# Conditioning row of the first projection: whole rows of 2048 columns ahead of the weights, and a counter of four

## Chip, cores and metric

One core of one Trainium2 chip. The metric is the device time of one execution in microseconds, taken as the median of several runs.

## What is computed

Two transformer-like blocks run one after the other on 256 tokens of width 1024. Only the head of the first block matters here: a condition vector `c` makes a shift and a scale for the tokens, and the modulated tokens are projected to queries, keys and values.

```
def ada_modulation(c, w, b):
    mod = jax.nn.silu(c) @ w + b
    shift, scale, gate = jnp.split(mod, 3, axis=-1)
    return shift[:, None, :], scale[:, None, :], gate[:, None, :]
...
        shift, scale, gate = ada_modulation(c, ada_w[i, 0], ada_b[i, 0])
        h = x * (1.0 + scale) + shift
        if i % N_MIXERS == 0:
            y = windowed_gqa(h, attn_w_in[j], attn_w_out[j], attn_sinks[j])
```

`ada_w[0, 0]` has 1024 rows of 3072 columns. Shift and scale are its first 2048 columns (8 MB); `attn_w_in` has 1024 rows of 1536 columns (6 MB).

## The kernel before, in words

**The weights' stream.** A `Stream` object `W` holds a list of items in the order of their use. An item is either a weight block (`add`) or a filler with a function of its own (`fill`). `load_to` (line 176) issues each item's DMA on SyncE's queue into one of `NSTAGE = 5` staging tiles `stg` of 1 MB. `split_to` (line 196) divides a weight block into a rounded part `wh` (ScalarE, line 217) and a rest `wl` (VectorE, line 222), in halves of up to 1024 columns, so that `mm3` (lines 389 to 391) can multiply in three passes. `step` (line 228) takes the next item: it loads up to five items ahead, splits blocks that are near, and for a filler calls its function, which multiplies the tile that has landed.

**The first projection.** `ada0(c)` (line 656) makes, for each c of 0 to 7, a filler with the 256 columns of `ada_w` that modulate the 128 channels c: 128 of the shift and 128 of the scale. Its DMA has runs of 128 floats, 512 bytes each. The filler multiplies with `cS` (the condition after silu, as 32 columns of which one is filled) on TensorE (line 671) into `adaps`, and VectorE copies the result to `adaR` (line 673). The items alternate: filler c, block c of `attn_w_in` (768 KB).

In `project` (line 1083) TensorE goes through c = 0 to 7. For each c, `modulate(c)` turns the row of `adaR` into two columns by two small matmuls (line 1075), adds the bias (line 1077), applies them to the transposed tokens `xT` on ScalarE (line 1079), and makes the pair `hH`, `hL` on VectorE (lines 1080, 1081). Then come 18 matmuls of 512 columns: 6 for keys and values (into `gen`) and 12 for queries (into `acc`). `turn_in` transposes the tokens (line 1059). Pieces of another job, the filters `hy` of the second block (lines 976 and 994), are put in at c = 4, 5, 6 and 7. The order of TensorE is the order of the program; the orders of the other engines come from a scheduler.

**After the projection.** The attention follows, and inside it eight fillers of whole rows (line 433) for the next shift and scale, which `fin_ss` hands to `row_cols` (line 485). That sends the row from `adaR` (VectorE, line 440) to DRAM and back as columns `adaC` by two DMAs on GpSimd's queue (lines 489 and 490), and puts the use of the columns (`sst`, lines 569 to 573) on a list with a counter:

```
        GP.dma_start(flat, R[row:64 * n:32, :])
        GP.dma_start(C[:, :n, :], flat.rearrange("(s r) (p k) -> s (r p) k", s=n, k=8).rearrange("s p k -> p s k"))
        W.due.append([LAG, lambda: use(C)])
```

Each `step` counts it down; below zero the use is put into the program. `gate_sums` (line 506) sums partial products for the gate on TensorE (line 502) and adds them to a tile `gate` on VectorE (line 503).

Of the kernel before, what the change touches and what calls it, by code (L numbers as in the profile page):

```python
# [11 lines left out]
F32 = mybir.dt.float32  # L12
F32R = mybir.dt.float32r
I32 = mybir.dt.int32
AF = mybir.ActivationFunctionType
OP = mybir.AluOpType
# [17 lines left out]
GROUPS = [(0,), (1, 2), (3, 4), (5, 6)]  # L34
RANK = [6, 7, 8, 9, 0, 2, 3, 1, 4, 5, 10, 11, 12, 13]
NSTAGE, NPART, NMORE = 5, 4, 6
LAG = 2
QSCALE = float(HD ** -0.5)


# [238 lines left out]
def tile_model(ctx: ExitStack, tc: tile.TileContext, A, out):  # L279
    nc = tc.nc  # L280
    PE, V, SC, GP = nc.tensor, nc.vector, nc.scalar, nc.gpsimd
    cst = ctx.enter_context(tc.tile_pool(name="cst", bufs=1))
# [3 lines left out]
    sml = ctx.enter_context(tc.tile_pool(name="sml", bufs=2))  # L286
    rows = ctx.enter_context(tc.tile_pool(name="rows", bufs=4, space=bass.MemoryType.DRAM))

    W = Stream(tc, stage, parts, NSTAGE, 1)
# [19 lines left out]
    one = K("ones")  # L309
# [14 lines left out]
    cS = cst.tile([128, 8, 32], F32, name="cS")  # L324
    cS2 = cst.tile([128, 8, 32], F32, name="cS2")
    V.memset(cS, 0.0)
    V.memset(cS2, 0.0)
    epsc = cst.tile([128, 3], F32, name="epsc")
    V.memset(epsc[:, 0:1], 1e-5)
    V.memset(epsc[:, 1:2], 1e-6)  # L330
    csil = cst.tile([128, 3, 8], F32, name="csil")
# [65 lines left out]
    psC = pes.enter_context(tc.tile_pool(name="psC", bufs=1, space=PSUM))  # L397
# [4 lines left out]
    def gen():  # L402
        return psB.tile([128, 512], F32, name="gen")
# [233 lines left out]
    def collect(jobs):  # L637

        keep, W.items = W.items, []
        for j in jobs:  # L640
            j()
        got, W.items = W.items, keep
        return got
# [8 lines left out]
            done = want  # L652


    ADA0 = {}
    VCH = ()

    def ada0(c):
        def fn(t):
            tv = t.rearrange("p (j n) -> p j n", j=8)  # L660
            if c in VCH:
                R = sml.tile([128, 256], F32, name="adaQ")
                V.tensor_scalar(R, tv[:, 0, :], csil[:, 0, 0:1], None, op0=OP.mult)
                for j in range(1, 8):
                    V.scalar_tensor_tensor(R, tv[:, j, :], csil[:, 0, j:j + 1], R, op0=OP.mult, op1=OP.add)
                ADA0[c] = R
                return
            ps = psC.tile([128, 512], F32, name="adaps")
            for j in range(8):
                g = j % 4  # L670
                PE.matmul(ps[32 * g:32 * g + 32, :256], cS[:, j, :], tv[:, j, :], start=(j < 4), stop=(j >= 4))
            R = sml.tile([128, 512], F32, name="adaR", bufs=1)
            V.tensor_copy(R[:, :256], ps[:, :256])
            ADA0[c] = R

        ap = A["ada_w"][0, 0][:, 0:2048].rearrange("(p j) (s c n) -> c p j s n", j=8, s=2, n=128)[c]
        W.fill("ada", ap, fn)

    wv, wo = rview("attn_w_in", 0), rview("attn_w_out", 0)
    for k in range(8):  # L680
        ada0(k)
        W.add("attn_in", wv[:, k, :])
    fl = collect([ADA1[0, 1][0], ADA1[0, 0][3]])
    for m in range(4):
        n0, n1 = ((0, 6), (6, 8), (8, 10), (10, 12))[m]
# [345 lines left out]
        hps.close()  # L1031


    W.load_to(1)
    late_loads()

    def attention():
        aes = ExitStack()
        ap = aes.enter_context(tc.tile_pool(name="attn", bufs=1, reuse_waits="tile"))
# [13 lines left out]
        def turn_in(first):  # L1053
# [14 lines left out]
            V.tensor_copy(badd[:, 0], pv[:, 0])  # L1068
            V.tensor_scalar(badd[:, 1], pv[:, 1], 1.0, None, op0=OP.add)

        def modulate(c):
            R = ADA0.pop(c)
            ps = gen()
            for s in range(2):
                PE.matmul(ps[:, s:s + 1], R[:, 128 * s:128 * s + 128], one, start=True, stop=True)
            ab = sml.tile([128, 2], F32, name="ab0")
            V.tensor_add(ab, ps[:, 0:2], badd[:, :, c])
            v = ip.tile([128, 256], F32, name="v0", bufs=2)
            SC.activation(v, xT[:, c, :], AF.Identity, bias=ab[:, 0:1], scale=ab[:, 1:2])
            V.tensor_copy(hH[:, c, :], v)  # L1080
            V.tensor_sub(hL[:, c, :], v, hH[:, c, :].bitcast(F32))

        def project(hy):
            W.step()
            turn_in(True)
            kv = [gen(), gen()]
            modulate(0)
            
            qa = [[accb(), accb()], [accb(), accb()]]
            for c in range(8):  # L1090
                w = W.next("attn_in")
                (qh, ql), (kh, kl) = w.parts

                def rows(ps, t, wh, wl):
                    ts = slice(128 * t, 128 * t + 128)
                    mm3(ps, (hH[:, c, ts], hL[:, c, ts]), (wh, wl), c == 0, c == 7)

                if 0 < c < 7:
                    W.step()
                for t in range(2):  # L1100
                    rows(kv[t], t, kh, kl)
                if c == 0:
                    turn_in(False)
                    W.step()
                if c < 7:
                    modulate(c + 1)
                for g in range(2):
                    sl = slice(512 * g, 512 * g + 512)
                    for t in range(2):
                        rows(qa[g][t], t, qh[:, sl], ql[:, sl])  # L1110
                for _ in range((0, 1, 0, 0, 1, 1, 1, 1)[c]):
                    next(hy)
                if c == 6:
                    nc.sync.dma_start(amask, A["c_amask"])
            return kv, qa
# [1452 lines left out]
```

## Time and profile before

| | us |
|---|---|
| median of 3 runs | 1212.63 (1207.86 to 1213.87) |
| the profiled execution | 1208.85 |
| its span | 1206.8 |
| TensorE busy in the span | 1125.0 (93%) |
| VectorE busy | 776.7 (64%) |
| ScalarE busy | 551.3 (46%) |
| the large DMA queue, share of 16 engines | 70.9% |

The rows below come from the profiled execution. Its own time is 3.8 us under the median of the runs. Times in a timeline count from the start of the span. In a row, `[1.10 <-DVE adaR L673]` says that the engine was idle for 1.10 us before and what ended it.

### The profile page before, as it was taken

The numbers are of one execution on the slowest core, as the hardware profiler recorded it, in microseconds if no ns is written. First come the engines' busy times: TensorE is split into PE (matmuls) and PEld (weight loads), VectorE is DVE, ScalarE is ACT, GpSimd is POOL, SyncE is SP. The second block draws the span as 40 slices with busy tenths as digits, with TensorE's granted clock in tenths as the row PEclk, the third lists the DMA queues.
The fourth block names the chain that finished last, engine by engine and source line by source line (L and its number), as shares of the span: only waits on it lengthen the run. The fifth ranks groups of instructions, "written<-read, shape, count | busy, mean of one in ns | idle before, by whom it ended". The sixth has DMA issues, their size and how long they took to land. (4 is left out here: it accounts for less than half of the span.)

```text
span 1206.8 us, 17360 instructions
## 1 busy us (share of the span) xinstructions
PE 1125.0 (93%) x6618; PEld 821.0 (68%) x6618; DVE 776.7 (64%) x1458; ACT 551.3 (46%) x934; POOL 103.9 (9%) x177
## 2 busy tenths in 40 slices
PE   5999799999989999989999999999999898999974
PEld 3657598989866576548889988888988533335321
DVE  4588788888575885597788769968798621112112
ACT  2456444454457677745445545753665410102111
POOL 6000271000013120010000000100000000000000
PEclk9999899999989999989999999999999999999998
DMA  9988598988694572468879876564326889999994
GB/s 287 323 323 302 187 316 310 331 299 300 208 261 145 164 203 68 146 225 318 284 258 315 279 239 204 186 207 140 123 96 213 356 345 420 420 420 382 342 407 173
DMA packets 146050, 317.57 MB, mean 263 GB/s; under 512 B 8402, under 2 KB 97730, under 8 KB 129576
## 3 DMA queue, kind: packets, MB, share of 16 engines
q1 hardware_dynamic: 138744, 304.17, 70.9%
q0 software_dynamic: 7216, 12.22, 3.3%
q8 instruction: 54, 0.88, 0.3%
q14 instruction: 36, 0.29, 0.1%
HBM read 315.27 MB, written 1.09 MB: 262 GB/s over the span
## 5 line engine op out<-in xcount | busy, mean ns | idle before, releaser
L217 ACT ACTIVATE wh<-stg 128x1024 fp32r<-128x1024 f32 x236 | 241.2, 1042 | 192.4 <-issue 71.3
L222 DVE TENSOR_TENSOR wl<-stg,wh 128x1024 fp32r<-128x1024 f32 x233 | 276.9, 1206 | 72.8 <-ACT wh L217 70.1
L391 PE MATMUL gen<-hH,wl 128*128 128x256 f32 x704 | 198.4, 282 | 4.6 <-DVE wl L222 4.6
L389 PE MATMUL gen<-hH,wh 128*128 128x256 f32 x704 | 199.6, 284 | 3.0 <-ACT hH L847 2.0
L390 PE MATMUL gen<-hL,wh 128*128 128x256 f32 x704 | 197.9, 282 | 1.0 <-DVE hL L851 1.0
L389 PEld LDWEIGHTS gen<-hH,wh 128*128 128x128 f32 x704 | 135.2, 192 | 10.8 <-ACT hH L847 5.3
L391 PEld LDWEIGHTS gen<-hH,wl 128*128 128x128 f32 x704 | 135.1, 192 | 7.3 <-DVE wl L222 7.3
L390 PEld LDWEIGHTS gen<-hL,wh 128*128 128x128 f32 x704 | 135.1, 192 | 2.9 <-POOL zp L1454 0.8
L389 PE MATMUL acc<-wh,mH 128*128 128x512 f32 x256 | 101.2, 395 | 0.0
L391 PE MATMUL acc<-wh,mL 128*128 128x512 f32 x256 | 100.7, 393 | 0.0
L390 PE MATMUL acc<-wl,mH 128*128 128x512 f32 x256 | 100.5, 393 | 0.0
L466 DVE SCALAR_TENSOR_TENSOR adav<-stg,csil,adav 128x1024 f32<-128x1024 f32 (+2 forms) x56 | 79.3, 1415 | 11.6 <-DMA stg<-in_ada_w_dram 10.8
L2393 PE MATMUL mgu<-stg,wl 128*32 128x512 f32 (+2 forms) x256 | 64.4, 625 | 7.1 <-DMA stg<-in_moe_w_up_dram 7.1
L2428 PE MATMUL mmi<-stg,mhT 128*32 128x512 f32 (+2 forms) x256 | 59.1, 598 | 7.3 <-DMA stg<-in_moe_w_down_dram 5.7
L2393 PE MATMUL mgu<-stg,wh 128*32 128x512 f32 (+2 forms) x256 | 64.4, 613 | 0.0
L1499 PE MATMUL gen<-xr,bd 128*128 128x256 f32 (+1 forms) x224 | 60.3, 411 | 1.4 <-DVE xr L1475 1.4
L2438 DVE TENSOR_TENSOR mhid<-mmi,gate 128x512 f32<-128x512 f32 x14 | 9.6, 689 | 80.2 <-PE mmi L2428 80.2
L389 PEld LDWEIGHTS acc<-wh,mH 128*128 128x128 f32 x256 | 48.1, 188 | 11.6 <-issue 0.8
L391 PEld LDWEIGHTS acc<-wh,mL 128*128 128x128 f32 x256 | 48.1, 188 | 10.9 <-issue 0.8
L390 PEld LDWEIGHTS acc<-wl,mH 128*128 128x128 f32 x256 | 48.1, 188 | 10.3 <-DVE wl L222 0.6
L2398 DVE SCALAR_TENSOR_TENSOR mhid<-mgu,mws,mhid 128x512 f32<-128x512 f32 x7 | 5.3, 750 | 70.0 <-PE mgu L2393 70.0
L2393 PEld LDWEIGHTS mgu<-stg,wl 128*32 128x32 f32 (+2 forms) x256 | 18.8, 134 | 44.5 <-issue 32.0
(604 smaller groups left out, 2117.2 us busy)
## 6 DMA issues: line engine op xcount, KB each, us to landing
stg<-in_ada_w_dram SPq DMA_DIRECT2D x72, 1024.0 KB, 6.1
stg<-in_mlp_w_dram SPq DMA_DIRECT2D x64, 1024.0 KB, 6.8
stg<-in_moe_w_up_dram SPq DMA_DIRECT2D x32, 1024.0 KB, 11.0
stg<-in_moe_w_gate_dram SPq DMA_DIRECT2D x32, 1024.0 KB, 11.5
stg<-in_moe_w_down_dram SPq DMA_DIRECT2D x32, 1024.0 KB, 18.1
stg<-in_w_in_dram SPq DMA_DIRECT2D x20, 1024.0 KB, 5.4
stg<-in_rnn_w_in_dram SPq DMA_DIRECT2D x12, 1024.0 KB, 6.3
stg<-in_attn_w_in_dram SPq DMA_DIRECT2D x8, 768.0 KB, 10.3
```

The source lines that it names most:

```text
L217: nc.scalar.activation(h, t[:, sl], AF.Copy)
L222: sub()
L389: PE.matmul(o, ah, bh, start=first, stop=False)
L390: PE.matmul(o, ah, bl, start=False, stop=False)
L391: return PE.matmul(o, al, bh, start=False, stop=last)
L466: V.scalar_tensor_tensor(acc, tv[:, j, :], col[:, k:k + 1], acc, op0=OP.mult, op1=OP.add)
L1499: PE.matmul(pv[c0:c1, q, :], BD[g % 2][:, q, d, o:o + c1 - c0], xr[g][:, kt, :], start=(i == 0), stop=True, skip_group_check=True)
L2393: PE.matmul(ps[sl], gx[c][:, k, o + sl.start:o + sl.stop], t[:, 512 * k:512 * k + 512], start=first, stop=last)
L2398: V.scalar_tensor_tensor(hid, got[1], WS[w], hid, op0=OP.mult, op1=OP.mult)
L2428: PE.matmul(both[h][sl], hT[:, k, sl], t[:, o:o + 512], start=k == 0, stop=k == 3)
L2438: V.tensor_mul(gated, ps, MOD["g5"][:, 512 * h:512 * h + 512])
```

## The change

The eight fillers of 256 columns become eight of whole rows: filler kc holds 2048 columns of the rows 8p + kc, in runs of 8192 bytes, made by the same helper `ada_fill` that the later fillers use. All eight add into one `adaps`, so shift and scale are complete after the eighth only. The first seven stand ahead of the first block of `attn_w_in`, the eighth behind it. One set of four small matmuls with `pick` (four columns, each one on 32 partitions) turns the whole row into all 16 columns, and one addition adds the biases. The loads of the constants and tokens stand behind four tiles where they stood behind one. `LAG` goes from 2 to 4.

```diff
-LAG = 2
+LAG = 4
...
+    pick = cst.tile([128, 4], F32, name="pick")
+    V.memset(pick, 0.0)
+    for g in range(4):
+        V.memset(pick[32 * g:32 * g + 32, g:g + 1], 1.0)
...
-    ADA0 = {}
-    VCH = ()
-
-    def ada0(c):
...
-        ap = A["ada_w"][0, 0][:, 0:2048].rearrange("(p j) (s c n) -> c p j s n", j=8, s=2, n=128)[c]
-        W.fill("ada", ap, fn)
+    ADA0 = []
+    ada_fill("ada", cS, A["ada_w"][0, 0].rearrange("(p k) n -> p k n", k=8), 0, 512, ADA0.append)
+    last = W.items.pop()
 
     wv, wo = rview("attn_w_in", 0), rview("attn_w_out", 0)
     for k in range(8):
-        ada0(k)
         W.add("attn_in", wv[:, k, :])
+        if k == 0:
+            W.items.append(last)
...
-    W.load_to(1)
+    W.load_to(4)
     late_loads()
...
+        ab = ip.tile([128, 2, 8], F32, name="ab0")
+
+        def columns():
+
+            R = ADA0.pop()
+            ps = gen()
+            for k in range(4):
+                PE.matmul(ps[:, 4 * k:4 * k + 4], R[:, 128 * k:128 * k + 128], pick, start=True, stop=True)
+            V.tensor_add(ab.rearrange("p s (h k) -> p s h k", h=2),
+                         ps[:, 0:16].rearrange("p (k s h) -> p s h k", k=4, s=2),
+                         badd.rearrange("p s (h k) -> p s h k", h=2))
+
         def modulate(c):
-            R = ADA0.pop(c)
-            ps = gen()
-            for s in range(2):
-                PE.matmul(ps[:, s:s + 1], R[:, 128 * s:128 * s + 128], one, start=True, stop=True)
-            ab = sml.tile([128, 2], F32, name="ab0")
-            V.tensor_add(ab, ps[:, 0:2], badd[:, :, c])
             v = ip.tile([128, 256], F32, name="v0", bufs=2)
-            SC.activation(v, xT[:, c, :], AF.Identity, bias=ab[:, 0:1], scale=ab[:, 1:2])
+            SC.activation(v, xT[:, c, :], AF.Identity, bias=ab[:, 0, c:c + 1], scale=ab[:, 1, c:c + 1])
...
         def project(hy):
-            W.step()
-            turn_in(True)
+            for k in range(7):
+                W.step(0 if k < 6 else None)
+                if k == 5:
+                    turn_in(True)
+            turn_in(False)
+            w = W.next("attn_in", 0)
+            W.step(0)
+            columns()
             kv = [gen(), gen()]
             modulate(0)
...
             for c in range(8):
-                w = W.next("attn_in")
+                w = W.next("attn_in") if c else w
...
-                if 0 < c < 7:
-                    W.step()
                 for t in range(2):
                     rows(kv[t], t, kh, kl)
-                if c == 0:
-                    turn_in(False)
-                    W.step()
                 if c < 7:
                     modulate(c + 1)
```

What TensorE has at its start, before the change (`adaps` are the fillers, `acc<-csm,xnat` the transposes of tokens, `gen<-csm,adaR` the columns, `gen<-wh,hH` the first projection matmul):

```order
L671 MATMUL adaps<-stg,cS 32x256 x8
L1059 MATMUL acc<-csm,xnat 128x128 x4
L1066 MATMUL gen<-csm,brow 128x16
L1075 MATMUL gen<-csm,adaR 128x1 x2
L389 MATMUL gen<-wh,hH 128x512
```

and with the change, where `gen<-pick,adaR` makes all columns:

```order
L437 MATMUL adaps<-stg,cS 32x512 x24
L1044 MATMUL acc<-csm,xnat 128x128 x4
L1051 MATMUL gen<-csm,brow 128x16
L437 MATMUL adaps<-stg,cS 32x512 x4
L1044 MATMUL acc<-csm,xnat 128x128 x12
L437 MATMUL adaps<-stg,cS 32x512 x4
L1063 MATMUL gen<-pick,adaR 128x4 x4
L393 MATMUL gen<-wh,hH 128x512
```

The first projection matmul has moved from behind one filler to behind eight, and no filler or column matmul stands between the projection's matmuls any more.

On VectorE, with the change, the same place, from the copies of the transposed tokens to the first `hH`, `hL`:

```order
L1046 COPY xT<-acc 128x512
L222 TENSOR_TENSOR wl<-stg,wh 128x1024
L222 TENSOR_TENSOR wl<-stg,wh 128x512
L444 COPY adaR<-adaps 128x512
L1064 TENSOR_TENSOR ab_197<-gen,badd 128x16
L1071 CAST hH<-v_295 128x256
L1072 TENSOR_TENSOR hL<-v_295,hH 128x256
```

The rest of the first weight block (`wl`) stands ahead of the copy of the row, where before it stood behind `hH` and `hL`.

On VectorE, near the end of the attention, before the change (`sst` uses the columns `adaC`, `gate` frees a PSUM bank):

```order
L569 TENSOR_TENSOR sst<-adaC,adb 128x8
L570 SCALAR_TENSOR_TENSOR sst<-adaC,adb 128x8
L503 SCALAR_TENSOR_TENSOR gate<-gen,gate 128x512
L571 TENSOR_TENSOR ab_1083<-sst,gbc 128x8
L573 TENSOR_TENSOR ab_1083<-sst,gbc 128x8
L222 TENSOR_TENSOR wl<-stg,wh 128x1024
```

and with it:

```order
L573 TENSOR_TENSOR sst<-adaC,adb 128x8
L574 SCALAR_TENSOR_TENSOR sst<-adaC,adb 128x8
L575 TENSOR_TENSOR ab_1003<-sst,gbc 128x8
L577 TENSOR_TENSOR ab_1003<-sst,gbc 128x8
L576 TENSOR_TENSOR ab_1003<-ab_1003,sst 128x8
L507 SCALAR_TENSOR_TENSOR gate<-gen,gate 128x512
```

The use of the columns still stands ahead of the gate's sum, with three small operations more between them.

## Rows read from the trace of the kernel before

**Rows 1.** Four stretches: columns are stretch, busy us (count) by engine, clock, DMA share, GB/s.
```profile
2.00:4.00 2.00, 0.00 (x0) 0.00 (x0) 0.17 (x1) 0.24 (x2) 2.00 (x4) 1.00 0.54 131
20.00:30.00 10.00, 8.90 (x64) 6.40 (x63) 5.98 (x10) 4.83 (x7) 4.75 (x9) 1.00 1.16 318
60.00:70.00 10.00, 10.00 (x42) 7.22 (x42) 7.75 (x34) 3.85 (x9) 0.00 (x0) 1.00 1.02 422
70.00:80.00 10.00, 9.74 (x53) 4.77 (x53) 9.20 (x29) 3.99 (x7) 0.00 (x0) 1.00 0.43 150
```

**Rows 2.** Timeline of TensorE: start us, us, line, operation, count, idle before.
```profile
8.15 1.94 PE L671 MATMUL adaps<-stg,cS 128*32 128x256 f32 x16 [8.15 <-DMA stg<-in_ada_w_dram]
...
16.12 0.80 PE L389 MATMUL gen<-wh,hH 128*128 128x512 f32 x1 [2.35 <-ACT wh L217]
...
18.91 0.63 PE L390 MATMUL gen<-wl,hH 128*128 128x512 f32 x1
19.34 0.63 PE L391 MATMUL gen<-wh,hL 128*128 128x512 f32 x1
...
22.46 1.09 PE L671 MATMUL adaps<-stg,cS 128*32 128x256 f32 x16
...
64.67 1.12 PE L994 MATMUL gen<-hw,ha 64*128 64x512 f32 x2
65.72 0.50 PE L389 MATMUL gen<-wh,hH 128*128 128x512 f32 x1
66.06 0.40 PE L390 MATMUL gen<-wl,hH 128*128 128x512 f32 x1
...
69.73 0.40 PE L391 MATMUL acc<-wh,hL 128*128 128x512 f32 x1
70.06 2.84 PE L994 MATMUL gen<-hw,ha 64*128 64x512 f32 x6
```

**Rows 3.** DMA queues and issues, 0 to 30 us: KB each, us to landing.
```profile
q0 software_dynamic: 1088, 0.25, 5.5%
...
stg<-in_ada_w_dram SPq DMA_DIRECT2D x5, 1024.0 KB, 9.9
stg<-in_attn_w_in_dram SPq DMA_DIRECT2D x4, 768.0 KB, 11.8
xnat<-in_x_dram SPq DMA_DIRECT2D x2, 512.0 KB, 6.0
csm<-c_small_dram SPq DMA_DIRECT2D x1, 247.0 KB, 7.1
```

**Rows 4.** Timeline of all engines: from a row's product to its hH.
```profile
15.58 1.83 DVE L222 TENSOR_TENSOR wl<-stg,wh 128x1024 fp32r<-128x1024 f32 x2 [0.20 <-ACT wh L217]
...
24.18 0.42 DVE L673 COPY adaR<-adaps 128x256 f32<-128x256 f32 x1
24.65 0.61 PE L1075 MATMUL gen<-csm,adaR 128*128 128x1 f32 x4 [1.10 <-DVE adaR L673]
...
26.12 0.29 DVE L1080 CAST hH<-v 128x256 fp32r<-128x256 f32 x1 [0.67 <-ACT v L1079]
...
74.76 1.07 PE L433 MATMUL adaps<-stg,cS 128*32 128x512 f32 x8
```

**Rows 5.** Timelines of VectorE and TensorE at the attention's end.
```profile
112.50 0.66 DVE L440 COPY adaR<-adaps 128x512 f32<-128x512 f32 x1
...
124.59 0.17 DVE L569 TENSOR_TENSOR sst<-adaC,adb 128x8 f32<-128x8 f32 x1 [4.72 <-DMA adaC<-flat]
...
124.75 0.69 DVE L503 SCALAR_TENSOR_TENSOR gate<-gen,gate 128x512 f32<-128x512 f32 x1
...
120.61 1.89 PE L1188 MATMUL gen<-PT,vN 128*128 128x256 f32 x8
125.50 3.39 PE L1188 MATMUL gen<-PT,vN 128*128 128x256 f32 x8 [3.00 <-DVE gate L503]
```

**Rows 6.** Timeline of ScalarE in the attention.
```profile
95.00 1.06 ACT L217 ACTIVATE wh<-stg 128x1024 fp32r<-128x1024 f32 x1
```

More of the change, by code (lines that the diff above doesn't have):

```diff
@@ L652, in spread @@
             done = want
-    ADA0 = {}
-    VCH = ()
-    def ada0(c):
[L659 to L674, printed above, removed]
-        ap = A["ada_w"][0, 0][:, 0:2048].rearrange("(p j) (s c n) -> c p j s n", j=8, s=2, n=128)[c]
-        W.fill("ada", ap, fn)
+    ADA0 = []
+    ada_fill("ada", cS, A["ada_w"][0, 0].rearrange("(p k) n -> p k n", k=8), 0, 512, ADA0.append)
+    last = W.items.pop()
     wv, wo = rview("attn_w_in", 0), rview("attn_w_out", 0)
     for k in range(8):
-        ada0(k)
         W.add("attn_in", wv[:, k, :])
+        if k == 0:
+            W.items.append(last)
     fl = collect([ADA1[0, 1][0], ADA1[0, 0][3]])
```

## The prediction

> **What bounds the kernel now.** I read the busy times of stretches first, then TensorE's timeline at the start, then the DMA queues of the first 30 us, then the chain of engines behind one row, and last the end of the attention, where the counter could act. In the stretch of 20 to 30 us TensorE is busy 8.90 of 10 us and at 60 to 70 all of it, while the DMA engines are full as well [rows 1]. So the first projection is bound by TensorE once it has begun. Before that TensorE waits for data: its first work starts when the first tile lands, at 8.15 [rows 2]. The place to compare is the end of the projection: its last matmul is followed at 70.06 by a piece of the filters [rows 2]. What comes behind starts from the same state in both kernels (the same items are up to five tiles ahead), so a shift of this point is a shift of everything behind, unless a queue order changes there.
>
> **What is removed.** Seven fillers between the projection's matmuls at 1.1 us each and seven sets of column matmuls at 0.4 to 0.6 [rows 2, 4]: 7 x 1.1 + 7 x 0.5 = 11 us of TensorE. The 12 transposes of tokens between the blocks move ahead of the projection too. In return the projection can't begin before the eighth tile has landed, been multiplied, and been turned into columns. The question is whether the late start eats what the dense run gives.
>
> **When the eighth tile lands.** Ahead of it and with it go eight tiles of 1024 KB, one block of 768 KB, two halves of tokens of 512 KB and constants of 247 KB [rows 3]: 8.39 + 0.79 + 1.05 + 0.25 = 10.5 MB (10^6 bytes). The rate is the first unknown, because the trace has no whole rows at its start. The nearest row for the form of the transfer is the stretch 60 to 70, where fillers of whole rows come in: 422 GB/s. The nearest for the place is 20 to 30, with 512-byte runs among the blocks: 318 [rows 1]. I take 420, by the form: in both stretches the engines are full, so the difference lies in what they carry. 10.5 / 0.420 = 25.0 us. The stream begins at about 3.1, since 2 to 4 us had moved 131 x 2 = 262 KB [rows 1], 0.9 us of work. GpSimd's small loads take 5.5% of 30 us [rows 3], 1.65 us, if they displace the stream, and 0 if they go beside it; I take all of it, and 0.4 for landing. Eighth tile: 3.1 + 25.0 + 1.65 + 0.4 = 30.2.
>
> The Trainium skill, "DMA: Bandwidth & Descriptors", Specifications, says that transfers reach line rate from 512 bytes on. By that rule the change of runs brings no rate, the tiles come at 318 as the pieces did, and the sum would be about 8 us worse. The two stretches above differ by a third with full engines, which speaks against the rule here; they also lie 40 us apart with other traffic.
>
> **From there to the first matmul.** The eighth filler: 1.07, as the filler of the same shape at 74.76 [rows 4] (1.94 if TensorE is at its lower level, as at 8.15 [rows 2]). Then the chain of one row, measured before from the copy at 24.18 to the end of the rounded part, 26.12 + 0.29 = 26.41, so 2.23 [rows 4]; the copy of 512 columns in place of 256 costs 0.66 - 0.42 = 0.24 more [rows 4, 5], and four column matmuls in place of two about 0.5 more [rows 4]. VectorE has the rest of the first block ahead of the copy, two subtractions of 1.83 together [rows 4]. That block lands one tile earlier, so they may be over or not: 0 to 1.83, and I take 0.5, since 2.5 us of transfer lie between. Sum 1.07 + 2.23 + 0.24 + 0.5 + 0.5 = 4.5. First matmul at 30.2 + 4.5 = 34.7, against 16.12 before [rows 2].
>
> **The dense run.** Block 7 stands alone in the trace: 16 of its 18 starts lie between 66.06 and 69.73, 3.67 / 16 = 0.229 apart [rows 2]. 8 x 18 x 0.229 = 33.0. The filters' piece at c = 6 takes 65.72 - 64.67 = 1.05 [rows 2]; those at c = 4 and 5 have half the columns, 0.55 each as an estimate from it, and each switch of kind costs 0.1 before and behind (0.34 at 65.72, 0.33 at 69.73 in place of 0.23 [rows 2]), 0.6 for three. Together 33.0 + 2.15 + 0.6 = 35.8. VectorE keeps up: 1.83 for a split, 0.29 for `hH` [rows 4] and, being of the same size, not much more for `hL`, in 4.1 us per block; weights of 0.79 MB arrive in 1.9 us. End of the projection: 34.7 + 35.8 = 70.5, which is 0.4 later than 70.06.
>
> **TensorE's clock at that start.** Before, the matmuls of 512 columns at 18.91 lasted 0.63, 0.43 apart, where later ones lasted 0.40, and at 22.46 a filler took 1.09 that had taken 1.94 at 8.15 [rows 2]. That is half the rate, so 1.2 GHz, though the clock column has 1.00; between lay some 6 us of nearly unbroken work. If the projection begins at the lower level and needs the same 6.3 us (16.1 to 22.4) to leave it, 6.3 / 0.43 = 14.7 matmuls are 0.20 longer each: 2.9 us. If the work ahead of the projection has done that already, 0. I take 0: from the seventh filler on (its tile lands with 8.65 MB, at 3.1 + 20.6 + 2.05 = 25.7) TensorE has that filler, 12 transposes, the eighth filler and the columns, nearly unbroken up to 34.7.
>
> The Trainium skill, "TensorE: Matmul & The Clock Gate", "HAM oscillation — how this bites in real kernels", says that bursts shorter than the transfer they wait for leave the array at the lower level. Fillers of 1 us every 2.5 us are that, so by it the 2.9 would be paid in full; no row before shows such a train.
>
> **The counter.** `LAG` sets when the use of columns enters the program, but VectorE's order is the scheduler's. With the change `sst` still stands right ahead of the gate's sum, and with 2 in place of 4 the changed kernel's rows are the same on all five engines. So this part doesn't do what it says: 0, from both sides. The stall stays: the copy at 112.50, two DMAs, `sst` at 124.59, the gate at 124.75, and TensorE idle 3.00 until 125.50 [rows 5].
>
> **Moves behind.** SyncE issues three loads of `gate` of 0.5 MB ahead of the sixth filler of the attention instead of later. They fall where the queue runs dry: 150 GB/s at 70 to 80 [rows 1]; 0. If they met the fillers instead, 1.57 / 0.42 = 3.7 us of queue. ScalarE does two halves of an output weight of 1.06 each [rows 6] ahead of a copy that frees a bank where it did them behind: between 0 (they fill a wait) and 2.1; 0. GpSimd's order is unchanged. The new memsets lie in VectorE's first microseconds, before the condition arrives: 0. Constants and tokens behind four tiles land by about 17 us (5.5 MB) and are wanted behind the sixth filler: 0 while the fillers cover them, else TensorE waits for them there.
>
> **Sum.** +0.4 us on the profiled execution: 1208.85 + 0.4 = 1209.3. That execution stands 3.8 under the median of the runs, so for the median 1212.6 + 0.4 = **1213.0**. A measurement here tells about 0.5%, 6 us, from no change; this is within.
>
> **Rivals.**
> - *Slower: the tiles come at the old rate.* 10.5 / 0.318 = 33.0 in place of 25.0, the eighth tile lands at 38, and all behind moves by 8.0: 1221. It decides from a landing at 36 on, 6 us over my sum's point (a rate under 340). For it: the place, and GpSimd's loads in the same time. Against: full engines at 422 with the same form [rows 1]. With 2.9 for the clock a milder rate does it. 0.14. The rule on 512 bytes in the Trainium skill, "DMA: Bandwidth & Descriptors", would make this the case.
> - *Faster: the stall at 122.5 goes after all.* If VectorE reaches the copy earlier or the two DMAs are quicker, TensorE's 3.00 idle go and the 3.39 that follow return to 1.89 [rows 5]: 4.5 us. With GpSimd's loads beside the stream (1.65) and no wait for the subtractions (0.5) the sum is 0.4 - 6.65 = -6.2: 1206.4. Against: the order on VectorE still has the wait ahead of the gate, and TensorE reaches it after the same work. 0.06.
> - *The clock: the projection starts at the lower level.* 0.4 + 2.9 = 3.3: 1215.9, not told from no change. For it: a filler of 1 to 2 us in each 2.5 us of transfer before. Against: the nearly unbroken work from 25.7 on. 0.25. The Trainium skill, "TensorE: Matmul & The Clock Gate", would make this the case.
> - *The counter doesn't act:* above; by the order this is so, and it is in the forecast.
>
> **How the numbers follow.** My case has 0.55 and the clock's 0.25; both lie within 0.5%, 0.80 together. Its bounds are -1.65 for GpSimd's loads, -0.5 to +1.3 for the subtractions, 0 to 2.1 on ScalarE, 0.9 for a slow eighth filler and part of the stall. The 80% range takes it with some of the slower rival and the spread of runs: 1207 to 1220. Faster by over 0.5% 0.06, within 0.80, slower 0.14.
>
> **What would show it.** Right: whole-row tiles at over 400 GB/s from 4 to 28 us; the eighth filler at about 30; the first projection matmul at 34 to 35; starts 0.23 apart up to 70 to 71; the row's copy to `sst` again some 12 us, with TensorE idle about 3 before the last `PT` product. Wrong: a rate near 320, matmuls 0.43 apart well into the first block, idle time between blocks, or a stall that is gone.

## The result, and the profile of the changed kernel

The changed kernel takes **1227.02 us** (median of four runs, 1224.77 to 1230.64); the kernel before, run again beside it, 1213.25. The ratio is **1.0127, 95% interval 1.0095 to 1.0159**: 15.4 us slower, between 11.5 and 19.3 (the two medians of four, taken as they stand, are 13.8 apart). The forecast was 1213.0, no change, with a range up to 1220. It is wrong. It gave 0.14 to this side, but for another cause: the rival had the tiles at the old rate and the eighth landing at 36 or later, and it landed by 32.0.

| | before | after |
|---|---|---|
| median of the runs, us | 1213.25 | 1227.02 |
| profiled execution, its span, us | 1208.85, 1206.8 | 1224.77, 1222.7 |
| first projection's first matmul, us | 16.12 | 37.36 |
| first projection's end, us | 70.06 | 76.69 (+6.6) |
| ScalarE near the end (line 2505, now 2496), us | 1183.78 | 1199.54 (+15.8) |

So there are two losses: 6.6 us up to the projection's end, and 9 more between there and the end of the program.

**The front.** The busy times of seven stretches of the changed kernel, in the columns of [rows 1]:

```profile
0.00:32.00 32.00, 13.71 (x73) 3.17 (x73) 5.72 (x27) 4.44 (x8) 19.59 (x39) 0.84 0.95 352
16.00:20.00 4.00, 1.50 (x8) 0.00 (x0) 0.00 (x0) 0.00 (x0) 2.85 (x7) 0.50 1.06 392
20.00:30.00 10.00, 6.83 (x41) 2.40 (x41) 1.51 (x4) 1.12 (x2) 5.24 (x10) 0.71 1.03 398
25.70:34.70 9.00, 5.63 (x39) 2.59 (x36) 4.04 (x7) 2.54 (x4) 0.64 (x2) 0.88 1.02 401
32.00:36.00 4.00, 3.20 (x16) 1.89 (x16) 0.98 (x2) 0.00 (x0) 0.00 (x0) 0.57 1.02 418
36.00:40.00 4.00, 2.77 (x7) 2.19 (x8) 3.07 (x7) 3.05 (x5) 0.00 (x0) 0.50 1.02 412
44.00:48.00 4.00, 4.00 (x19) 3.22 (x18) 2.85 (x6) 3.17 (x5) 0.00 (x0) 1.00 0.70 224
```

Whole rows came at 398 GB/s in 20 to 30 us, where the 512-byte runs had 318 [rows 1], but not at the 420 that I took; the 28 us from 4 to 32 have 386 on average. TensorE, with 1.50 us of work in 16 to 20, was granted 0.50 of its clock (1.2 GHz), and again in 36 to 40, as the projection begins; in 44 to 48 it was granted all of it (2.4 GHz). TensorE's own timeline, as [rows 2]:

```profile
7.68 3.94 PE L437 MATMUL adaps<-stg,cS 128*32 128x512 f32 x16 [7.68 <-DVE cS L338]
...
22.05 1.94 PE L437 MATMUL adaps<-stg,cS 128*32 128x512 f32 x8 [4.55 <-DMA stg<-in_ada_w_dram]
...
32.00 1.47 PE L437 MATMUL adaps<-stg,cS 128*32 128x512 f32 x8 [2.28 <-DMA stg<-in_ada_w_dram]
34.27 1.87 PE L1063 MATMUL gen<-pick,adaR 128*128 128x4 f32 x8 [0.79 <-DVE adaR L444]
37.36 0.80 PE L393 MATMUL gen<-wh,hH 128*128 128x512 f32 x1 [1.23 <-DVE hH L1071]
37.96 0.63 PE L394 MATMUL gen<-wl,hH 128*128 128x512 f32 x1
...
42.22 0.63 PE L395 MATMUL acc<-wh,hL 128*128 128x512 f32 x1
42.65 0.45 PE L393 MATMUL acc<-wh,hH 128*128 128x512 f32 x1
42.94 0.40 PE L394 MATMUL acc<-wl,hH 128*128 128x512 f32 x1
...
76.69 2.84 PE L979 MATMUL gen<-hw,ha 64*128 64x512 f32 x6
```

The eighth filler starts at 32.00, the projection at 37.36. Its first twelve matmuls are spaced 0.43 us (37.36 to 42.65) as those at the lower level were in [rows 2], and from 42.65 on they are 0.2335 apart on average. The DMA queues of 0 to 30 us and VectorE's chain, as [rows 3, 4]:

```profile
q0 software_dynamic: 1079, 0.25, 4.9%
...
stg<-in_ada_w_dram SPq DMA_DIRECT2D x8, 1024.0 KB, 14.4
```

```profile
30.46 1.83 DVE L222 TENSOR_TENSOR wl<-stg,wh 128x1024 fp32r<-128x1024 f32 x2 [0.44 <-ACT wh L217]
33.52 0.69 DVE L444 COPY adaR<-adaps 128x512 f32<-128x512 f32 x1 [1.24 <-PE adaps L437]
...
37.01 0.29 DVE L1071 CAST hH<-v 128x256 fp32r<-128x256 f32 x1 [0.67 <-ACT v L1070]
```

The two subtractions were over 1.24 us before the copy could start, so they cost nothing in this execution.

**The stall at the attention's end** stayed, as forecast. VectorE's and TensorE's rows for [rows 5]:

```profile
118.73 0.68 DVE L444 COPY adaR<-adaps 128x512 f32<-128x512 f32 x1
...
132.04 0.17 DVE L573 TENSOR_TENSOR sst<-adaC,adb 128x8 f32<-128x8 f32 x1 [7.08 <-DMA adaC<-flat]
...
132.60 0.68 DVE L507 SCALAR_TENSOR_TENSOR gate<-gen,gate 128x512 f32<-128x512 f32 x1
```

```profile
133.34 1.99 PE L1179 MATMUL gen<-PT,vN 128*128 128x256 f32 x8 [2.91 <-DVE gate L507]
```

From the copy to `sst` are 13.3 us (12.1 before), TensorE idles 2.91 (3.00). The product behind it starts 7.84 later than before and takes 1.99 where it took 3.39, so behind this place the program is 6.4 us late, as it was ahead of it.

**The rest of the program** has the same work and loses 9 us more. It doesn't lose them evenly: ScalarE's rows, matched in order and taken by their median over 50 us, are 6.8 us late from 100 us on, 12.2 from 300, still 11.8 from 600, 18.1 from 900 and 15.8 at the end. One row of ScalarE among the experts, before and after:

```profile
1183.78 0.58 ACT L2505 ACTIVATE mgu<-macc 128x512 f32<-128x512 f32 x1 [10.47 <-PE macc L2454]
```

```profile
1199.54 0.58 ACT L2496 ACTIVATE mgu<-macc 128x512 f32<-128x512 f32 x1 [8.97 <-PE macc L2445]
```

TensorE's waits have not grown (its gaps of over 0.15 us from 140 us on add up to 51 us before and 44 after), and the granted clock of the dense stretches from 550 to 750 us is 1.00 in both. What has grown is the spacing of the matmuls. In the MLP, on TensorE, the same run of 256-column matmuls, first before (13 spaces from the first row to the last) and then after (14 spaces):

```profile
230.05 0.28 PE L389 MATMUL gen<-hH,wh 128*128 128x256 f32 x1
...
231.52 0.28 PE L390 MATMUL gen<-hL,wh 128*128 128x256 f32 x1
```

```profile
239.27 0.28 PE L393 MATMUL gen<-hH,wh 128*128 128x256 f32 x1
...
240.95 0.28 PE L395 MATMUL gen<-hH,wl 128*128 128x256 f32 x1
```

1.47 / 13 = 0.113 us before, 1.68 / 14 = 0.120 after, with the same duration (0.28) of each in the record: a group's mean duration doesn't show it, only the starts do. Over the whole program the mean space is 0.1144 before and 0.1193 after for 256 columns (some 2000 spaces), and 0.2290 and 0.2326 for the 512 columns of the MLP's second product (some 730). With 2112 of the one and 768 of the other, 2112 x 4.9 ns + 768 x 3.6 ns = 13 us, part of which falls where TensorE waits anyway.

### The profile page after: what moved, and what is told of

It is laid out like the page before. It is cut to its first block, busy times and chain, and to the rows that moved or that the text cites. A ratio compares the mean times of both kernels' runs of the same rounds, so it can differ in the third digit from the quotient of the medians.

```text
span 1222.7 us, 17174 instructions
## 1 busy us (share of the span) xinstructions
PE 1136.5 (93%) x6530; PEld 827.6 (68%) x6530; DVE 775.4 (63%) x1449; ACT 551.8 (45%) x934; POOL 104.2 (9%) x177
## 5 line engine op out<-in xcount | busy, mean ns | idle before, releaser
L395 PE MATMUL gen<-hH,wl 128*128 128x256 f32 x704 | 201.1, 286 | 2.2 <-DVE wl L222 2.2
L437 PE MATMUL adaps<-stg,cS 128*32 128x512 f32 x256 | 41.7, 689 | 19.1 <-DMA stg<-in_ada_w_dram 11.4
L393 PEld LDWEIGHTS acc<-wh,mH 128*128 128x128 f32 x256 | 48.2, 188 | 12.2 <-ACT mH L1297 0.8
L395 PEld LDWEIGHTS acc<-wh,mL 128*128 128x128 f32 x256 | 48.2, 188 | 12.1 <-issue 0.8
```

What stands on the lines that cost most here:

```text
L393: PE.matmul(o, ah, bh, start=first, stop=False)
L395: return PE.matmul(o, al, bh, start=False, stop=last)
L437: PE.matmul(st["ps"][32 * g:32 * g + 32, :n], cs[:, k, :], tv[:, j, g, :], start=(k == 0), stop=(k == 7))
```

## The experiments

One thing that the change does beside its work is not in any instruction: its tile `pick` takes 32 bytes per partition in the pool of constants, ahead of the weights, and `ab0` leaves the pool of small tiles (64 bytes), ahead of the activations. All weight tiles (`stg`, the parts `wh` and `wl`) so begin 32 bytes further on, and all activations (`hH`, `hL`, the MLP's `mH`, `mL`, the mixers' and the experts' tiles) 32 bytes further back. My first theory was that tiles are to begin at a multiple of 64 bytes. The places below are those of the built programs.

### Where the tiles lie: e1_pick64, e2_pad32, e3_act32, e4_wts32

```diff
-    pick = cst.tile([128, 4], F32, name="pick")
+    pick = cst.tile([128, 16], F32, name="pick")[:, 0:4]
```

> The changed kernel with its new tile pick given a 64-byte slot, of which 16 bytes are used as before: nothing else is edited, but every tile that lies behind it in SBUF begins 64 bytes on from where the kernel before has it (the tiles of the activations at the very address of before), and so at a multiple of 64 bytes again, where the change as made has them 32 bytes off one. Theory (places of tiles): the matmuls' spacing goes back from 0.2327 to 0.229 us (512 columns) and from 0.119 to 0.1145 (256 columns), the later part of the loss (+6.6 us at the projection's end growing to some +16) goes, the front's +6 stays: 1218 to 1220 us, ratio to the kernel before about 1.005. Rival (the spacing comes from the transfers, the clock or the instructions' own places in memory): spacing and time as in the changed kernel, some 1227 us, ratio about 1.013.

The other three are the kernel before with tiles that nothing reads: `padc` alone, `pads` alone, and both.

```diff
+    pad = cst.tile([128, 4], F32, name="padc")
+    V.memset(pad, 0.0)
+    pads = sml.tile([128, 4], F32, name="pads", bufs=1)
+    V.memset(pads, 0.0)
     epsc = cst.tile([128, 3], F32, name="epsc")
```

> The kernel before with a tile of 16 bytes (a 32-byte slot) that nothing reads, at the place where the change puts pick: all tiles behind it, weights, their parts and activations, begin 32 bytes further on. Order and work are else those of before. Theory (places of tiles): the first projection ends where it did within 1 us, from there on the matmuls are spaced 0.2327 and 0.119 us, and the kernel loses 8 to 11 us, 1221 to 1224. Rival: no change, 1213 within 2.

> The kernel before with the 32-byte tile in the pool of small tiles instead: weights and their parts (stg, wh, wl) stay where they are, the activations (hH, hL, xrH, MH and what lies behind) begin 32 bytes further on. If the place of the activations is what slows the matmuls, this has all the loss of e2_pad32 (8 to 11 us); if that of the weights and parts, nothing (within 2 us of before); if each adds its share, about half.

> The kernel before with both 32-byte tiles: weights and parts begin 32 bytes further on, activations 64 bytes further on and so at multiples of 64 again. If the place of the weights and their parts slows the matmuls, all of e2_pad32's loss (8 to 11 us); if that of the activations, nothing; about half if each adds its share.

| | weights, bytes | activations, bytes | first `hH` less first `wh` | 256 columns, us | 512 columns, us | ratio (95%) |
|---|---|---|---|---|---|---|
| before | 0 | 0 | 48576 | 0.1144 | 0.2290 | 1 |
| the change | +32 | -32 | 48512 | 0.1193 | 0.2326 | 1.0127 (1.0095 to 1.0159) |
| e1_pick64 | +64 | 0 | 48512 | 0.1189 | 0.2323 | 1.0095 (1.0060 to 1.0131) |
| e2_pad32 | +32 | +32 | 48576 | 0.1142 | 0.2291 | 0.9994 (0.9970 to 1.0018) |
| e3_act32 | 0 | +32 | 48608 | 0.1183 | 0.2332 | 1.0081 (1.0054 to 1.0108) |
| e4_wts32 | +32 | +64 | 48608 | 0.1183 | 0.2332 | 1.0090 (1.0060 to 1.0120) |

My theory fell twice: e1_pick64 has everything at multiples of 64 and stays slow, e2_pad32 has nothing there and is as quick as before. So did its rival, since a 32-byte tile without any change of order costs 0.8% (e3_act32). What e2_pad32 shares with the kernel before is the distance between weights and activations; e3_act32 and e4_wts32 share one with each other, and their spacing. The new theory: the distance between the two operands of a matmul counts, not where either lies.

### The distance, alone and undone: e5_dist_back, e8_before_dist, e6_act128

e5_dist_back is the changed kernel with 64 unread bytes ahead of the activations, e8_before_dist the kernel before with the change's places, e6_act128 the kernel before with 128 bytes ahead of the activations.

```diff
+    spare = sml.tile([128, 16], F32, name="spare", bufs=1)
+    V.memset(spare[:, 0:4], 0.0)
     epsc = cst.tile([128, 3], F32, name="epsc")
```

> The changed kernel with a 64-byte tile in the pool of small tiles that nothing reads: the weights stay 32 bytes further on than in the kernel before, the activations come to lie 32 bytes further on too, so that the distance from the first weight part (wh) to the first activation tile (hH) is 48576 bytes again as before (48512 in the change). Theory (the distance between the two operands of a matmul sets its spacing): 0.229 and 0.1145 us again, and the loss is the front's alone: 5 to 7 us over the kernel before, ratio 1.004 to 1.006. Rival (it is something else that the changed kernels share: longer transfers, other instruction counts): spacing 0.233 and 0.119, ratio 1.0095 to 1.013 as in the changed kernel and in e1_pick64.

```diff
+    padc = cst.tile([128, 4], F32, name="padc")
+    V.memset(padc, 0.0)
     epsc = cst.tile([128, 3], F32, name="epsc")
...
-            ab = sml.tile([128, 2], F32, name="ab0")
+            ab = ip.tile([128, 2], F32, name="ab0", bufs=2)
```

> The kernel before, its order untouched, with the change's places: a 32-byte tile where pick lies, and ab0 moved from the pool of small tiles into that of xT, so that the weights begin 32 bytes further on and the activations 32 bytes further back (distance 48512). Theory (distance): first projection within 1 us of before, spacing 0.233 and 0.1195, loss 8 to 11 us, ratio 1.007 to 1.009, that is the change's loss without the front. Rival (the growing loss comes with the change's order): ratio 1.000.

> The kernel before with 128 bytes more ahead of the activations; the weights stay. The distance is 48704 bytes, which leaves 64 when divided by 128, as the 48576 of before does; e1_pick64 (48512) and e3_act32 and e4_wts32 (48608) leave 0 and 96. Theory (what counts is the distance modulo 128): time and spacing of before, ratio 1.000 within 0.003. Rival (only the distance of before is good, or a longer period counts): spacing 0.233 and 0.119, ratio 1.008 to 1.010.

| order | distance | 256 columns, us | 512 columns, us | ratio (95%) |
|---|---|---|---|---|
| changed | before's (e5_dist_back) | 0.1142 | 0.2290 | 1.0041 (1.0009 to 1.0074) |
| before's | the change's (e8_before_dist) | 0.1193 | 0.2324 | 1.0085 (1.0056 to 1.0114) |
| both changed | (the change) | 0.1193 | 0.2326 | 1.0127 (1.0095 to 1.0159) |

This is the answer to the whole result: the order costs 0.41% (5.0 us, between 1.1 and 9.0), the places 0.85% (10.3 us, between 6.8 and 13.8), together 15.3 where 15.4 were seen. With such intervals the close match is partly luck; that both are there, and that the places cost the more by their middle values, is what the runs show. In e5_dist_back the projection ends at 74.91 us, 4.85 later than before. A single trace can't settle the shares: ScalarE's row of 1183.78 stands at 1194.79 in that of e5_dist_back, 11.0 late, but at 1191.58, 7.8 late, in that of e10_act256 below, which has the order and the spacing of before. e6_act128 (48704) came out at 1.0076 (1.0047 to 1.0104), spacing 0.1175 and 0.2334: bytes modulo 128 are not it.

### How far the distance repeats: e9_act512, e10_act256, e11_act_less32, e15_act160

The kernel before each time, with `spare` of 512, 256 or 160 bytes ahead of the activations; in e11_act_less32 the weights go 32 bytes up and the activations stay (e8_before_dist with 32 bytes of `spare`).

> The kernel before with 512 bytes more ahead of the activations, the weights unmoved: distance 49088 bytes, the same modulo 512 as the 48576 of before, and another modulo 1024. Theory (the distance counts modulo 512 or less): spacing 0.229 and 0.1145, time of before, ratio 1.000 within 0.003. Rival (a longer period, or only the very distance of before is good): 0.233 and 0.118, ratio 1.007 to 1.009.

> The same with 256 bytes: distance 48832, the same as before modulo 256 and not modulo 512. Theory (modulo 256): spacing and time of before, ratio 1.000 within 0.003. Rival (modulo 512 or longer): 0.233 and 0.118, ratio 1.007 to 1.009.

> The kernel before with the weights 32 bytes further on and the activations where they were: distance 48544, between the good 48576 and the bad 48512. If only the distance of before is good: 0.233 and 0.119, ratio 1.007 to 1.009. If good distances form a stretch that reaches below 48576: the spacing of before or a shorter one, ratio 1.000 or under.

> The kernel before with 160 bytes more ahead of the activations, the weights unmoved: distance 48736, which leaves 96 modulo 256, the one multiple of 32 not seen so far. If only 192 is good: spacing 0.233 and 0.118, ratio to before 1.007 to 1.009. If 96 is as good or better than 192: 0.229 and 0.1145 or less, ratio 1.000 or under.

e9_act512: 1.0004 (0.9981 to 1.0028); e10_act256: 1.0002 (0.9980 to 1.0025); e11_act_less32: 1.0055 (1.0035 to 1.0076); e15_act160: 1.0102 (1.0074 to 1.0130). Two stretches of TensorE's timeline, 512 columns of the MLP, first e10_act256 (8 spaces), then e6_act128 (18 spaces):

```profile
260.14 0.39 PE L391 MATMUL acc<-wh,mH 128*128 128x512 f32 x1
...
261.97 0.39 PE L393 MATMUL acc<-wh,mL 128*128 128x512 f32 x1
```

```profile
259.65 0.39 PE L392 MATMUL acc<-wl,mH 128*128 128x512 f32 x1
...
263.85 0.39 PE L392 MATMUL acc<-wl,mH 128*128 128x512 f32 x1
```

1.83 / 8 = 0.2288 with 256 bytes more, 4.20 / 18 = 0.2333 with 128. So the distance counts modulo 256. Some tiles (`yH` of the recurrence, `H3` of the context, the experts' `Sg`) lie at other distances than `hH` in each kernel, which fills a table. The distance is the moving operand's place less the stationary one's, modulo 256; the rows are mean spaces in us:

| distance | 256 columns | 512 columns |
|---|---|---|
| 0 | 0.1190 (`Sg` over `xrH`, before) | 0.2287 (`wh` over `yH`, e11_act_less32) |
| 32 | 0.1166 (`H3` over `wh`, before) | 0.2332 (e3_act32) |
| 64 | 0.1175 (e6_act128) | 0.2290 (before) |
| 96 | 0.1199 (e15_act160) | 0.2334 (e11_act_less32) |
| 128 | 0.1193 (e8_before_dist) | 0.2324 (e8_before_dist) |
| 160 | 0.1183 (e11_act_less32) | 0.2339 (e15_act160) |
| 192 | **0.1144** (before) | 0.2334 (e6_act128) |
| 224 | 0.1183 (e3_act32) | 0.2334 (`wh` over `yH`, before) |

In the 256-column products the activations move over stationary weights, in the 512-column ones the weights move over stationary activations, so a change of place turns the sign. The kernel before has the two at 192 and 64, the best of the one column and within 0.3 ns of the best of the other.

### A version with the rest at good distances: e16_rest

```diff
+        pady = rw.tile([128, 40], F32, name="pady", bufs=1)
+        V.memset(pady[:, 0:4], 0.0)
...
     L3 = cp.tile([128, 8, 256], F32R, name="L3")
+    padh = cp.tile([128, 24], F32, name="padh")
+    V.memset(padh[:, 0:4], 0.0)
...
+    padg = gw.tile([128, 48], F32, name="padg", bufs=1)
+    V.memset(padg[:, 0:4], 0.0)
```

> The kernel before with three tiles that nothing reads, which move the pairs that lie at bad distances there: H3 and L3 begin 96 bytes lower (distance to wh 192 modulo 256 and not 32), yH and yL 160 bytes higher (192, not 32), Sg 192 bytes higher (192 from xrH, not 0); hH, mH, MH and the weights stay. Theory (the distance modulo 256): matmuls of H and wh with 256 columns from 0.1166 to 0.1145 us apart and with 512 columns from 0.2332 to 0.229 (725 to 800 us), those of yH from 0.2334 to 0.229, those of Sg from 0.1190 to 0.1145, together 192 x 2.3 ns + 48 x 4 ns + 144 x 4.3 ns + 96 x 4.5 ns = 1.7 us under the kernel before, ratio 0.9986, which five rounds can't tell from 1. Rival (those pairs are slow for another reason): spacing unchanged, ratio 1.000.

The table foretold each within 1.1 ns: `H3` with 256 columns 0.1166 to 0.1135 and with 512 columns 0.2332 to 0.2291, `yH` 0.2334 to 0.2294, `Sg` 0.1190 to 0.1156. `hH` and `mH`, which did not move, kept 0.1142 and 0.2294, so the pace goes by the pair of operands of each matmul and not by the kernel's places as a whole. TensorE's rows of `H3`'s 512 columns, ten spaces each, before and in e16_rest (0.233 and 0.229):

```profile
735.70 0.40 PE L390 MATMUL gen<-wl,H 128*128 128x512 f32 x1
...
738.03 0.40 PE L391 MATMUL gen<-wh,L 128*128 128x512 f32 x1
```

```profile
734.71 0.39 PE L391 MATMUL gen<-wh,L 128*128 128x512 f32 x1
...
737.00 0.39 PE L389 MATMUL gen<-wh,H 128*128 128x512 f32 x1
```

The time is 1209.52 against 1212.53, ratio 0.9975 (0.9955 to 0.9995). That is the only version of this study that is faster than the kernel before, by little: 1.7 us were worked out, and the interval goes from 0.6 to 5.5. The spaces are the evidence here; the time alone would hardly be one.

### What the order costs: e7_busy, e12_busy_less, e13_small_late, e14_both

All four start from e5_dist_back, so the distance is the good one and only the front is in play. First the clock: matmuls that nothing reads in TensorE's idle time.

```diff
+            def idle(n):
+                pd = accb()
+                for _ in range(n):
+                    PE.matmul(pd[:32, :256], cS[:, 0, :], cS.rearrange("p k n -> p (k n)"), start=True, stop=True)
+
             for k in range(7):
                 W.step(0 if k < 6 else None)
+                idle(5)
...
             W.step(0)
+            idle(4)
             columns()
+            idle(4)
```

> e5_dist_back with matmuls that nothing reads put into TensorE's idle time ahead of the projection: five of 128x256 behind each of the first seven tiles' fillers, four behind the eighth's and four behind the columns. Theory (the projection's first matmuls ran 0.43 us apart because TensorE had been idle for most of 12 to 37 us and the granted clock was 0.50): the clock is 1.00 at the projection's start, its first 12 matmuls are 0.23 apart, and the time is 2 to 4 us under e5_dist_back. Rival (the clock stays low whatever goes ahead, or the added matmuls delay the chain by as much): no gain, within 1 us of e5_dist_back or over it.

> e7_busy with fewer of the matmuls that nothing reads (three behind each of the first five tiles, one behind the next two, two behind the eighth and two behind the columns), since those of e7_busy put off the projection's start from 36.96 to 39.34 us, while its first matmuls ran 0.23 apart at once. Theory (clock and start can both be had): the projection starts at 36.7 to 37.4 us with 0.23 apart, ends at 73.0 to 73.8 us (74.91 in e5_dist_back, 75.73 in e7_busy), and the time is 1 to 2 us under e5_dist_back, ratio to before 1.002 to 1.004. Rival (fewer matmuls don't hold the clock): first matmuls 0.43 apart, no gain over e5_dist_back.

The stretch of 36 to 40 us and TensorE's first projection matmuls in e5_dist_back:

```profile
36.00:40.00 4.00, 3.04 (x7) 2.43 (x8) 3.30 (x7) 3.16 (x6) 0.00 (x0) 0.63 1.02 413
```

```profile
36.96 0.74 PE L395 MATMUL gen<-wh,hH 128*128 128x512 f32 x1 [1.23 <-DVE hH L1073]
...
40.06 0.58 PE L396 MATMUL acc<-wl,hH 128*128 128x512 f32 x1
40.48 0.39 PE L397 MATMUL acc<-wh,hL 128*128 128x512 f32 x1
```

and in e7_busy:

```profile
36.00:40.00 4.00, 4.00 (x22) 2.44 (x21) 2.39 (x7) 1.87 (x4) 0.00 (x0) 1.00 1.01 415
```

```profile
39.34 0.50 PE L395 MATMUL gen<-wh,hH 128*128 128x512 f32 x1
39.67 0.39 PE L396 MATMUL gen<-wl,hH 128*128 128x512 f32 x1
```

With TensorE at work all the time the clock is granted in full (2.4 GHz) and the first matmuls are 0.23 apart, so the idle front is what had it at the lower level (1.2 GHz). The theory is right on the clock and wrong on the gain: the added matmuls stood ahead of the chain and put the start off by 2.4 us, and the projection ended at 75.73. e12_busy_less, with half of them, keeps the rate and puts the start off by 0.5:

```profile
37.47 0.50 PE L395 MATMUL gen<-wh,hH 128*128 128x512 f32 x1 [0.25 <-DVE hH L1073]
...
73.85 2.84 PE L981 MATMUL gen<-hw,ha 64*128 64x512 f32 x6
```

It ends 1.1 us before e5_dist_back, just past the slow edge of what the theory said (73.0 to 73.8). The times alone don't tell it: 1.0028 (0.9997 to 1.0058) and 1.0028 (1.0009 to 1.0047), against 1.0041.

Then the rate: GpSimd's loads are held behind a copy that waits for the columns.

```diff
+    def small_loads():
+        held = GP.tensor_copy(spare[:, 0:16], MOD["ab"].rearrange("p s k -> p (s k)"))
+        with tc.issue_after(held.ins):
+            GP.dma_start(nr[:, 0], A["norm1_g_2"][0].rearrange("(p k) -> p k", k=8))
...
+            channel_loads()
...
             columns()
+            MOD["ab"] = ab
+            small_loads()
```

> e5_dist_back with 27 of GpSimd's small loads (those of nr, gbc, adb, adb2 and the channel vectors) held behind a copy on GpSimd that reads the columns of ab, so that they start at some 35 us and not from 2 to 22 us. Theory (the small loads take the rate from the tiles): 4 to 28 us run at 405 to 420 GB/s, the eighth tile's products start at 30.4 to 31.2 us and not at 32.16, the projection at 35.2 to 36.2, and the time is 0.8 to 1.8 us under e5_dist_back, ratio to before 1.002 to 1.004. Rival (they don't): rate 385 to 395, eighth tile within 0.4 us of 32.1, time as e5_dist_back.

> e12_busy_less with the same small loads held back. If small loads and clock each cost what the theories say: projection's start at 35.5 to 36.5 us with 0.23 apart, its end at 72.0 to 73.0 us (73.85 in e12_busy_less, 70.06 before), ratio to before 1.001 to 1.003, so still not faster than before. Rival (the small loads cost nothing): end at 73.5 to 74.2, ratio 1.002 to 1.004 as e12_busy_less.

Two stretches and the chain on VectorE in e13_small_late, and behind them the chain in e5_dist_back:

```profile
8.00:12.00 4.00, 2.74 (x16) 0.20 (x8) 0.71 (x4) 0.21 (x1) 0.00 (x0) 1.00 0.89 337
...
20.00:24.00 4.00, 1.38 (x8) 0.20 (x8) 0.00 (x0) 0.00 (x0) 0.00 (x0) 1.00 1.02 422
```

```profile
32.59 1.83 DVE L222 TENSOR_TENSOR wl<-stg,wh 128x1024 fp32r<-128x1024 f32 x2 [0.45 <-ACT wh L217]
34.33 0.68 DVE L458 COPY adaR<-adaps 128x512 f32<-128x512 f32 x1
```

```profile
32.20 1.83 DVE L222 TENSOR_TENSOR wl<-stg,wh 128x1024 fp32r<-128x1024 f32 x2 [0.44 <-ACT wh L217]
33.94 0.68 DVE L446 COPY adaR<-adaps 128x512 f32<-128x512 f32 x1
```

From 16 to 28 us the rows now come at 420 to 422, where e5_dist_back had 386 to 403. SyncE's queue moved 5.05 MB in that stretch and 4.61 in e5_dist_back: while GpSimd loads, the tiles lose some 9%. But six other loads of GpSimd (the router's weights among them) moved up into 4 to 12 us, where the rate fell to 357 and 337 from 395 and 383, so the eighth filler starts at 31.99 and not at 32.16. And the two subtractions stand in front of the row's copy, from 32.59 to 34.33, as they did in e5_dist_back from 32.20 to 33.94. They wait for the split on ScalarE, which stands behind a copy of the last transposes (30.11 here, 29.69 there); ahead of these TensorE works without a wait from the sixth filler on (25.11 here, 24.70 there), at the lower rate (1.94 us for a filler, though the clock column has 1.00 there). So in both it is the sixth tile and the low clock, not the eighth tile, that the row's copy hangs on. The projection ends at 75.35, 0.4 later than in e5_dist_back; the theory is right on the rate and wrong on what it brings by itself. In e14_both, beside the busy TensorE, it does bring something:

```profile
31.52 1.06 PE L451 MATMUL adaps<-stg,cS 128*32 128x512 f32 x8 [0.75 <-DMA stg<-in_ada_w_dram]
...
36.27 0.50 PE L395 MATMUL gen<-wh,hH 128*128 128x512 f32 x1 [0.25 <-DVE hH L1075]
...
72.67 2.84 PE L983 MATMUL gen<-hw,ha 64*128 64x512 f32 x6
```

The projection ends 1.2 us earlier than in e12_busy_less. Not all of that need be the loads': in that trace the eighth filler starts at 33.31, behind a wait of 2.48 for its tile, 1.1 later than in e5_dist_back, and no run shows why. The ratios are 1.0046 (1.0024 to 1.0068) for e13_small_late and 1.0019 (0.9999 to 1.0039) for e14_both. With most of both costs taken off, the change's order still ends the projection 2.6 us later than the kernel before.

## Why the prediction was wrong, point by point

**"A shift of this point is a shift of everything behind"** failed, and with the larger part: 10.3 of 15.4 us. The sentence was about instructions, queues and buffers, and those are the same behind the projection. But the new tile, of which I costed only the memsets (at 0), and the move of `ab0`, which I didn't cost at all, shift every tile of weights against every tile of activations by 64 bytes. e8_before_dist makes this shift alone and loses 0.85%; e5_dist_back takes it back, has the spacing of before, and loses 0.41%, which is the size of the front's 4.85 us. No rival had it.

**The rate of 420 GB/s** was mis-sized: 386 on average over 4 to 32 us. The choice by the form of the transfer was the nearer one (318 was the other end), but the row it came from, 60 to 70 us, has no GpSimd loads beside it; without them the tiles do come at 420 (e13_small_late). So the term of 1.65 for these loads had the right sign and was too small: they take a share of the rate for as long as they run. The 10.5 MB and the loads' own 0.25 are 27.9 us at 386, where 25.0 + 1.65 = 26.65 were taken. A second part was not in the sum: by 32.0 us 11.26 MB had moved (352 GB/s from 0 to 32), so some 0.5 MB of the blocks behind the eighth tile, issued from 24.05 on, went ahead of its end, 1.3 us. A little came back, since the stream was under way earlier than taken. The eighth filler started at 32.00, not at 30.2. On the rule of 512 bytes (the Trainium skill, "DMA: Bandwidth & Descriptors", Specifications) the traces stay against it: 318 with 512-byte runs [rows 1] and 398 with whole rows in the same 20 to 30 us, the engines full in both.

**The chain of 4.5** was 5.36: no wait for the subtractions (0, where 0.5 was taken; in e5_dist_back they did hold the copy up), but the eighth filler took 1.47 and the columns 1.87 at a lower clock. Together with the landing the first matmul came 2.7 later than forecast, at 37.36.

**The clock, taken at 0,** was the rival with 0.25 and it came true: twelve matmuls 0.43 apart took 5.3 us, 2.5 more than at 0.2335. "Nearly unbroken work from 25.7 on" was the step that failed: from 25.7 to 34.7 TensorE was busy 5.63 of 9 us, it idled 2.28 ahead of the eighth filler and 0.79 and 1.23 in the chain, and the granted clock of 32 to 36 us was 0.57. The prediction's own terms had the idle time: of its 4.5 us from the landing on, 2.23 are a chain in which TensorE mostly waits. e7_busy shows the cause. The Trainium skill ("TensorE: Matmul & The Clock Gate", "HAM oscillation — how this bites in real kernels") says so of bursts that are shorter than the transfers they wait for; the trace agrees, with 1.50 us of work and a clock of 0.50 in 16 to 20 us.

**The dense run** of 35.8 took 39.3: 2.5 for the clock, 0.65 for 144 spaces of 0.2335 in place of 0.229, which is the distance again, and 0.25 of a wait at 66.29 for ScalarE. Sum of the front: 0.4 forecast + 2.7 + 3.5 = 6.6, as seen.

**Right** were the stall that stays, the counter that does nothing (from the copy to `sst` 13.3 us, with the same order), the moves behind at 0 as far as the attention's end (6.6 us late at 70 us, 6.4 behind the stall), and that the dense run has no idle time between blocks to speak of.

## What to carry to other kernels

An edit that adds or drops a tile moves all tiles behind it, and on this kernel 64 bytes between weights and activations were worth some 10 us, about twice what the edit's own work cost: look up the tiles' places before and after, and keep the distance between the operands of the big matmuls (modulo 256 bytes) when you compare two versions. Where a loss grows with the clock at full rate and no wait growing, compare the starts of matmuls of one shape, not their durations. Work that waits for the last of a train of transfers paid three times here: for the rate under everything else that loads then, for the clock of an engine that idled, and for the chain behind the last one.

## What the runs showed that I had not expected

- The distance between a matmul's operands changes its pace: 0.1144 to 0.1199 us for 256 columns and 0.2287 to 0.2339 for 512, with a period of 256 bytes, and the good distances differ by shape: 192 for the one, 0 and 64 for the other. Where either operand begins (multiples of 64 or 32 off one) doesn't matter at equal distance. What inside the chip makes it so no run here shows.
- 32 bytes of unused space ahead of the activations cost 0.8% of a kernel of 1.2 ms, and 512, 256 or, with the weights moved alike, 32 cost nothing.
- Small loads by GpSimd, most of a few kilobytes and 0.25 MB in all, take some 9% of the rate from 1 MB tiles as long as they run (386 to 403 GB/s with them, their own bytes counted in, and 420 to 422 without).
